# Six MLP chunks with one pair of column blocks by seven products instead of eight

## The chip, the cores and the metric

The kernel runs on one core of a Trainium2 chip. The metric is the device time of one execution in microseconds; what is given for a kernel is the median of its runs. Five engines work beside each other, each through its own instructions in order: TensorE (PE, with the loads of its stationary operand shown as PEld), VectorE (DVE), ScalarE (ACT), GpSimd (POOL) and the queue that issues the loads, SyncE (SP).

## The reference

Two layers of a decoder over 256 tokens of width 2048, float32. Layer 0 mixes tokens with a gated unit, layer 1 with windowed attention. Behind either stands an MLP, and this is what the change touches:

```
def sq_relu_mlp(x, w_up, w_down):
    return jnp.square(jax.nn.relu(x @ w_up)) @ w_down

x = layer_norm(DEEPNORM_ALPHA * x + sq_relu_mlp(x, mlp_w_up[layer], mlp_w_down[layer]), ...)
```

`w_up` is 2048 x 8192 and `w_down` 8192 x 2048. So each MLP is an up product, relu and square, and a down product, added to a multiple of `x` ahead of a layer norm.

## The kernel before

**Precision and weight tiles.** Every float32 number is split into two float32r parts, high and low, and a product is the sum of three: high x high, high x low, low x high. All weights come in tiles of 128 x 1024 numbers in the order of their use. The class `Weights` loads a tile into one of four raw places (`RAW`), ACT casts it to its high part (L95), DVE subtracts that from the raw tile for the low part (L97), and both go to a place for parts: 5 (`SLOTS`) and, from the end of the token mixer to the end of the MLP, 5 more (`EXTRA_SLOTS`). `get` splits as many tiles ahead as there are places, loads four more, and hands out the next tile; `release` gives its place back. So the splits run up to nine tiles ahead of the products, and the cast for a place waits until PE has read the tile that was there.

**The MLP.** `mlp` goes through the 8192 features in four chunks of 2048. The up product of a chunk is 8 blocks of 256 features (`col_steps`: weights stationary, activations moving; a block of both token tiles needs four weight tiles). `act` takes a block: ACT copies one half of the bank (L294), DVE adds the other (L300), one DVE instruction does relu and square (L381), and `split` writes the high part (ACT, L185) and the low part (DVE, L186) to `hT`. The down product of the chunk is four column blocks of 512 (`rows_product`: activations stationary, weights moving). Each takes 8 weight tiles, and a tile means, for each of two token tiles, two K tiles of three matmuls of 512 columns (L205 to L207), twelve in all. `residual` then adds a column block to `x` (L353). The last column block of an MLP is `last_rows`, in which the layer norm of one token tile runs beside the products of the other; the first up tiles behind a norm are `skewed` likewise.

**Order.** Program order is a hint there: apart from the loads (always in the order of the program) and the subtractions around a layer norm, the framework's scheduler places the instructions of an engine. PSUM has two double banks with the tag `mm`, for the products, and two with the tag `aux`, for transposes, the gate and the attention. Two wide buffers (`wide`, in `bc`) hold the layer norm's gains and offsets.

Of the kernel before, what the change touches and what calls it, by code (L numbers as in the profile page):

```python
# [11 lines left out]
F32 = mybir.dt.float32  # L12
# [11 lines left out]
NFC = DFF // D  # L24
# [11 lines left out]
EXTRA_SLOTS = 5  # L36
# [10 lines left out]

class Weights:
    """The weights in the order of their use: each tile [128, 1024] is loaded and split
    into two float32r parts (high + low = the float32 value) ahead of its products."""  # L50

    def __init__(self, tc, pool, tiles):
        self.tc, self.nc, self.pool, self.tiles = tc, tc.nc, pool, tiles
        self.others, self.by_pool = [], ()
        self.borrowed, self.borrowed_from = [], 0
        self.raw, self.parts, self.held = {}, {}, []
        self.n_raw = self.n_split = self.n_used = 0
        self.free = {"w": SLOTS, "extra": 0}
        self.extra, self.extra_end = None, 0
# [23 lines left out]
    def ahead(self, n_split=None):  # L83
        """Split the tiles that have a place, and load the ones after them."""
        nc = self.nc
        n_split = len(self.tiles) if n_split is None else n_split
        while self.n_split < min(n_split, len(self.tiles)):
# [4 lines left out]
            self.load(self.n_split + 1)  # L92
            raw = self.raw.pop(self.n_split)
            for s in self.pieces(self.n_split):
                nc.scalar.copy(out=hi[:, s], in_=raw[:, s])  # L95
                engine = nc.gpsimd if self.n_split in self.by_pool else nc.vector
                sub = engine.tensor_tensor(out=lo[:, s], in0=raw[:, s], in1=hi[:, s].bitcast(F32),  # L97
                                           op=ALU.subtract)
                if self.in_order:
                    self.tc.keep_in_program_order(sub)  # L100
            self.parts[self.n_split] = (hi, lo, kind)
            self.n_split += 1
    def pieces(self, n):
        """The first tile goes in halves, so that the products start early."""
        return [slice(0, TILE // 2), slice(TILE // 2, TILE)] if n == 0 else [slice(0, TILE)]

    def load(self, n):
        while self.n_raw < min(n, len(self.tiles)):
            raw = self.pool.tile([P, TILE], F32, tag="w_raw", bufs=RAW, name="w_raw")
# [7 lines left out]
    def dma(self, out, in_):  # L117
        """Loads keep the order of the program: what is used first is loaded first."""
        self.tc.keep_in_program_order(self.nc.sync.dma_start(out=out, in_=in_))

    def get(self, ahead=None):
# [3 lines left out]
        self.load(self.n_split + RAW)  # L125
# [4 lines left out]
    def release(self):  # L130
        """The oldest tile in use has been used."""
# [6 lines left out]
def trunk(ctx: ExitStack, tc: tile.TileContext, t, out):  # L138
# [8 lines left out]

    def tiles_of(name):
# [3 lines left out]
    order = []  # L152
    ends = {}
    for name in ("win_v", "win_u", "wout", "mlp0", "kv", "wq", "wo", "mlp1"):
        tiles = (mlp_order(tiles_of("up" + name[3:]), tiles_of("down" + name[3:]))
                 if name.startswith("mlp") else tiles_of(name))
        if name == "wo":
            # the last heads' rows of the first two chunks come after the other rows of both
            tiles = tiles[0:6] + tiles[8:14] + tiles[6:8] + tiles[14:]
        order += tiles  # L160
        ends[name] = len(order)
    weights = Weights(tc, wpool, order)
    weights.by_pool = range(ends["kv"] + 4, ends["wq"], POOL_EVERY)
# [20 lines left out]
    def split(dst_hi, dst_lo, src):  # L184
        nc.scalar.copy(out=dst_hi, in_=src)  # L185
        nc.vector.tensor_tensor(out=dst_lo, in0=src, in1=dst_hi.bitcast(F32), op=ALU.subtract)  # L186

# [1 line left out]
    def row_steps(stat, apart=False):  # L189
        """[tokens, 512] of both token tiles: activations stationary, weights moving.  # L190
        One step for each weight tile and token tile."""
# [6 lines left out]
        def step(i, tok, hi, lo):  # L198
            for j in range(2):
                k = 2 * i + j  # L200
                wh, wl = hi[:, j * 512:(j + 1) * 512], lo[:, j * 512:(j + 1) * 512]
                xh = stat[:, k, tok * P:(tok + 1) * P]
                xl = stat[:, k, S + tok * P:S + (tok + 1) * P]
                first, last = k == 0, k == NK - 1
# [3 lines left out]
        return ps, [partial(step, i) for i in range(NK // 2)]  # L208

    def rows_product(stat):  # L210
        ps, steps = row_steps(stat)
# [78 lines left out]
    def gather_halves(ps, bias=None):  # L290
        """The sum of the two column halves of cols_product (with a bias per feature)."""
# [514 lines left out]
```

## Time and profile before

| | before |
|---|---|
| runs, us | 2007.83, 2011.8, 2012.14 (median 2011.8) |
| profiled execution: its span, us (no other time of it is given) | 2008.3 |
| PE busy | 98% |
| DVE busy | 62% |
| ACT busy | 46% |
| mean granted TensorE clock | 0.991 |

The span runs from the first to the last instruction of the profiled execution. Matmuls are pipelined, so that PE can be busy without being at its peak: the start of one matmul against the start of the next says more than its duration. Idle time is put down to what ended it, and idle time of an engine that is not the bottleneck costs nothing.

### The profile page before, as it was taken

What the parts mean: (1) busy time and instruction counts of PE and PEld (TensorE: products, weight loads), DVE (VectorE), ACT (ScalarE), POOL (GpSimd) and SP (SyncE); (2) the same over time, 40 slices, a digit from 0 to 9 for tenths busy, and PEclk for the clock granted to TensorE, in tenths of its full rate; (3) what the DMA queues carried; (4) which work ended last, traced back from release to release, by engine and by line L of the source; (5) the groups of instructions that cost most, each with busy time, mean ns of one, the idle gap of its engine ahead of it and who ended that gap; (6) DMA issues with size and microseconds to landing.
All of it is one profiled execution on the core that took longest, in us unless ns stands there. A gap on an engine that the chain in (4) does not pass through costs nothing.

```text
span 2008.3 us, 26243 instructions
## 1 busy us (share of the span) xinstructions
PE 1963.9 (98%) x10388; PEld 1685.8 (84%) x10388; DVE 1252.5 (62%) x1345; ACT 915.5 (46%) x1138; POOL 103.1 (5%) x63
## 2 busy tenths in 40 slices
PE   9999999999999999999998889999999999999997
PEld 7888888888888888888898878888888888888886
DVE  5676686555554655564778997965555555555555
ACT  5445445434443443443456675444344344434432
POOL 0000010000000000000133310100000000000001
PEclk9999999999999999999998899999999999999999
DMA  9754846666666666655543336566676666665653
GB/s 339 259 186 151 301 143 214 189 197 224 192 192 191 187 189 194 190 184 166 179 137 107 104 106 227 175 208 190 197 228 187 194 189 189 189 194 185 189 157 104
DMA packets 105963, 377.54 MB, mean 188 GB/s; under 512 B 12272, under 2 KB 12912, under 8 KB 105840
## 3 DMA queue, kind: packets, MB, share of 16 engines
q1 hardware_dynamic: 105840, 375.86, 59.4%
q8 instruction: 81, 1.33, 0.3%
q14 instruction: 42, 0.34, 0.0%
HBM read 373.72 MB, written 2.10 MB: 187 GB/s over the span
## 4 chain that ended last, share of the span: by engine, by line
issue 82%; PE 8%; DVE 6%; ACT 2%; POOL 2%; DMA 0%; SPq 0%; POOLq 0%; ACTq 0%; DVEq 0%
PE ps_r L205 2%; PE ps_r L206 2%; PE ps_r L207 2%; DVE w_lo L97 1%; ACT p L623 1%; PE ps_c L242 1%; PE ps_c L251 1%; DVE x L332 0%; DVE swap L544 0%; POOL rstd L313 0%; DVE pT L186 0%; POOL x L328 0%; POOL x L327 0%; DVE qT L697 0%; DVE x L330 0%
## 5 line engine op out<-in xcount | busy, mean ns | idle before, releaser
L97 DVE TENSOR_TENSOR w_lo<-w_raw,w_hi 128x1024 fp32r<-128x1024 f32 (+1 forms) x655 | 803.9, 1231 | 569.7 <-ACT w_hi L95 567.7
L95 ACT CAST w_hi<-w_raw 128x1024 fp32r<-128x1024 f32 (+1 forms) x669 | 701.3, 1051 | 760.3 <-PE ps_r L207 413.4
L205 PE MATMUL ps_r<-w_hi,hT 128*128 128x512 f32 x1024 | 398.5, 389 | 0.0
L207 PE MATMUL ps_r<-w_hi,hT 128*128 128x512 f32 x1024 | 398.5, 389 | 0.0
L206 PE MATMUL ps_r<-w_lo,hT 128*128 128x512 f32 x1024 | 398.4, 389 | 0.0
L246 PE MATMUL ps_c<-yT,w_hi 128*128 128x512 f32 x960 | 337.1, 398 | 0.0
L246 PE MATMUL ps_c<-oT,w_hi 128*128 128x512 f32 x960 | 337.1, 398 | 0.0
L251 PE MATMUL ps_c<-yT,w_lo 128*128 128x256 f32 x992 | 272.5, 281 | 0.0
L251 PE MATMUL ps_c<-oT,w_lo 128*128 128x256 f32 x992 | 272.5, 281 | 0.0
L207 PEld LDWEIGHTS ps_r<-w_hi,hT 128*128 128x128 f32 x1024 | 192.2, 188 | 40.0
L206 PEld LDWEIGHTS ps_r<-w_lo,hT 128*128 128x128 f32 x1024 | 192.2, 188 | 40.0
L205 PEld LDWEIGHTS ps_r<-w_hi,hT 128*128 128x128 f32 x1024 | 192.2, 188 | 39.5
L246 PEld LDWEIGHTS ps_c<-oT,w_hi 128*128 128x128 f32 x960 | 178.7, 188 | 41.8
L246 PEld LDWEIGHTS ps_c<-yT,w_hi 128*128 128x128 f32 x960 | 178.7, 188 | 41.8
L251 PEld LDWEIGHTS ps_c<-yT,w_lo 128*128 128x128 f32 x992 | 187.4, 189 | 2.7
L251 PEld LDWEIGHTS ps_c<-oT,w_lo 128*128 128x128 f32 x992 | 187.4, 189 | 2.7
L300 DVE TENSOR_TENSOR full<-ps_c,part 128x512 f32<-128x512 f32 x73 | 50.5, 691 | 91.5 <-ACT part L294 83.7
L294 ACT COPY part<-ps_c 128x512 f32<-128x512 f32 x72 | 42.2, 587 | 131.2 <-PE ps_c L246 128.5
L242 PE MATMUL ps_c<-hT,w_hi 128*128 128x256 f32 x512 | 97.8, 294 | 0.0
L313 POOL TENSOR_TENSOR rstd<-ve,half 128x1 f32<-128x1 f32 x10 | 9.9, 987 | 1709.1 <-DVE ve L311 1709.1
L246 PE MATMUL ps_c<-xT,w_hi 128*128 128x512 f32 x256 | 90.2, 396 | 0.0
L242 PEld LDWEIGHTS ps_c<-hT,w_hi 128*128 128x128 f32 x512 | 84.4, 203 | 0.4
(141 smaller groups left out, 2026.4 us busy)
## 6 DMA issues: line engine op xcount, KB each, us to landing
w_raw<-in_up SPq DMA_DIRECT2D x256, 512.0 KB, 4.2
w_raw<-in_down SPq DMA_DIRECT2D x256, 512.0 KB, 4.1
w_raw<-in_win_u SPq DMA_DIRECT2D x32, 512.0 KB, 4.0
w_raw<-in_wout SPq DMA_DIRECT2D x32, 512.0 KB, 4.4
w_raw<-in_wq SPq DMA_DIRECT2D x32, 512.0 KB, 3.6
w_raw<-in_wo SPq DMA_DIRECT2D x32, 512.0 KB, 4.0
w_raw<-in_win_v SPq DMA_DIRECT2D x31, 512.0 KB, 6.2
b_ln_g<-in_ln_g SPq DMA_DIRECT2D x8, 512.0 KB, 5.6
```

What stands on the lines that cost most here:

```text
L95: nc.scalar.copy(out=hi[:, s], in_=raw[:, s])
L97: sub = engine.tensor_tensor(out=lo[:, s], in0=raw[:, s], in1=hi[:, s].bitcast(F32), op=ALU.subtract)
L205: nc.tensor.matmul(out=ps[tok], lhsT=xh, rhs=wh, start=first, stop=False)
L206: nc.tensor.matmul(out=ps[tok], lhsT=xh, rhs=wl, start=False, stop=False)
L207: nc.tensor.matmul(out=ps[tok], lhsT=xl, rhs=wh, start=False, stop=last)
L242: nc.tensor.matmul(out=ps[:, b, 0:S], lhsT=hi[:, w], rhs=stat[:, k, h * S:(h + 1) * S], start=first and h == 0, stop=last and h == 1)
L246: nc.tensor.matmul(out=ps[:, b, :], lhsT=hi[:, w], rhs=stat[:, k, :], start=first, stop=last)
L251: nc.tensor.matmul(out=ps[:, b, 0:S], lhsT=lo[:, w], rhs=stat[:, k, 0:S], start=False, stop=False)
L294: nc.scalar.copy(out=part, in_=ps[:, :, S:])
L300: nc.vector.tensor_tensor(out=full, in0=ps[:, :, 0:S], in1=part, op=ALU.add)
L313: nc.gpsimd.tensor_tensor(out=rstd, in0=ve, in1=half, op=ALU.pow)
L623: nc.scalar.activation(out=p[:, i, :], in_=p[:, i, :], func=AF.Exp, bias=top[:, i:i + 1], accum_out=den[:, i:i + 1])
```

## The change

`CHUNKS` cuts the 8192 features of an MLP into six chunks of 1024 and one of 2048. The last is computed as before. In the six, the columns 0 to 1023 of the down product are a product of 2 x 2 blocks: two token tiles by K tiles of even and odd number, times those K tiles by two column blocks of 512. It is done with Strassen's seven products, as Winograd arranges the sums. A `group` is four K tiles; a chunk has two. The columns 1024 to 2047 remain plain.

- `down_steps` gives the order: products 0 to 3 of both groups, then 4 to 6 of both, with a plain weight tile behind every two of them. Each product has a bank of its own of `aux`: four in the first part, three in the second.
- `add_down` says which weights make each operand. `ahead` adds raw tiles in place on DVE, one addition ahead of the subtraction, for the operand behind; four of seven operands of a group bring an addition. B11 and B12 lie in the wide buffers, B22 and B21 in the raw ring. `end` tells when a raw tile is done with.
- `act` writes four sums of the activations beside the four plain blocks (`by_pairs` gives the layout of `hT`), and relu and square are two ACT instructions. It is cut into stages, one for each following `get`.
- `evict` adds three of the products to `x` itself; four are kept in `held` (copied by ACT in the first chunk, added to by DVE in the others) and combined by `strassen_end`, one addition for each block of the last up product.
- Inside the MLP DVE and ACT keep the order of the program (`tc.manual_schedule`). `EXTRA_SLOTS` goes from 5 to 4. Loads go as far ahead as raw places are free.

The weights in memory are put in the new order on the host (`down_tiles`). Comments and docstrings are removed. The core of the diff, blank lines left out:

```diff
-EXTRA_SLOTS = 5
+CHUNKS = ((1024, 1),) * 6 + ((2048, 0),)
+EXTRA_SLOTS = 4
+STATIONARY = (0, 7, 5, 4, 6, 2, 3)
+HELD = (0, 2, 3, 4)
...
+def down_steps(groups, rounds):
+    plain = [("plain", (n, i)) for n in range(2 * rounds, 4) for i in range(2 * groups)]
+    if not rounds:
+        return plain
+    steps = []
+    for part in (range(4), range(4, 7)):
+        steps += [("strassen", (g, o)) for g in range(groups) for o in part]
+    every = -(-len(steps) // len(plain))
+    out = []
+    for i, step in enumerate(steps):
+        out.append(step)
+        if (i + 1) % every == 0 and plain:
+            out.append(plain.pop(0))
+    return out + plain
...
-            self.load(self.n_split + 1)
-            raw = self.raw.pop(self.n_split)
+            at, add, ended = self.operands[self.n_split]
+            self.load(max((at,) + (add or ())) + 1)
+            raw = self.raw[at]
             for s in self.pieces(self.n_split):
                 nc.scalar.copy(out=hi[:, s], in_=raw[:, s])
+                if add is not None:
+                    into, plus = (self.raw[n] for n in add)
+                    nc.vector.tensor_tensor(out=into, in0=into, in1=plus, op=ALU.add)
...
+            if self.homes[self.n_raw] == "w":
+                if not self.free_raw:
+                    break
+                self.free_raw -= 1
+                raw = self.pool.tile([P, TILE], F32, tag="w_raw", bufs=RAW, name="w_raw")
+            else:
+                if not self.pairs or len(self.pairs[-1][1]) == 2:
+                    if len(self.pairs) == 2:
+                        break
+                    self.pairs.append((self.wide.tile([P, 2, TILE], F32, tag="wide", name="w_wide"),
+                                       [], []))
+                pair, began, _ = self.pairs[-1]
+                raw = pair[:, len(began)]
+                began.append(self.n_raw)
...
-        self.load(self.n_split + RAW)
+        self.load(len(self.tiles))
+        for stages in self.later:
+            stages.pop(0)()
+        self.later[:] = [stages for stages in self.later if stages]
...
+    def add_down(width, rounds, down):
+        groups = width // 512
+        at = {}
+        for kind, i in down_steps(groups, rounds):
+            if kind == "plain":
+                add_tiles([down.pop(0)])
+                continue
+            g, o = i
+            for name in {0: ("B11",), 1: ("B22", "B12"), 5: ("B21",)}.get(o, ()):
+                at[g, name] = len(tiles)
+                tiles.append(down.pop(0))
+                homes.append("wide" if name in ("B11", "B12") else "w")
+            b11, b12, b22, b21 = (at.get((g, name)) for name in ("B11", "B12", "B22", "B21"))
+            operands.append([(b11, None, ()),
+                             (b22, (b11, b12), ()),
+                             (b11, (b12, b22), ()),
+                             (b12, (b11, b22), (b12, b22)),
+                             (b11, None, ()),
+                             (b21, (b11, b21), (b21,)),
+                             (b11, None, (b11,))][o])
...
+    def strassen_steps(hT, groups, n, held, first, scale):
+        own = {1: (0, 1, ALU.subtract), 5: (0, 0, ALU.add), 6: (1, 0, ALU.add)}
+        banks = {}
+        def evict(o, bank):
+            if o in own:
+                tok, c, op = own[o]
+                a = x[:, tok, (n + c) * 512:(n + c + 1) * 512]
+                nc.vector.scalar_tensor_tensor(out=a, in0=a, scalar=scale, in1=bank,
+                                               op0=ALU.mult, op1=op)
+            elif first:
+                nc.scalar.copy(out=held[:, HELD.index(o), :], in_=bank)
+            else:
+                a = held[:, HELD.index(o), :]
+                nc.vector.tensor_tensor(out=a, in0=bank, in1=a, op=ALU.add)
+            if o == 6 and scale != 1.0:
+                a = x[:, 1, (n + 1) * 512:(n + 2) * 512]
+                nc.scalar.mul(out=a, in_=a, mul=scale)
+        def step(g, o):
+            if o not in banks:
+                two = psum.tile([P, 2, 512], F32, tag="aux", name="ps_s")
+                banks[o], banks[o + 1] = two[:, 0, :], two[:, 1, :]
+            hi, lo = weights.get()
+            for j in range(2):
+                k = 2 * g + j
+                wh, wl = hi[:, j * 512:(j + 1) * 512], lo[:, j * 512:(j + 1) * 512]
+                xh, xl = (hT[:, k, part, STATIONARY[o], :] for part in range(2))
+                start, stop = k == 0, k == 2 * groups - 1
+                nc.tensor.matmul(out=banks[o], lhsT=xh, rhs=wh, start=start, stop=False)
+                nc.tensor.matmul(out=banks[o], lhsT=xh, rhs=wl, start=False, stop=False)
+                nc.tensor.matmul(out=banks[o], lhsT=xl, rhs=wh, start=False, stop=stop)
+            weights.release()
+            if g == groups - 1:
+                evict(o, banks[o])
+        return step
...
+    def strassen_end(n, held):
+        m1, m5, m7, m6 = (held[:, i, :] for i in range(4))
+        (x11, x12), (x21, x22) = ([x[:, tok, (n + c) * 512:(n + c + 1) * 512] for c in range(2)]
+                                  for tok in range(NT))
+        for out, a, b, op in ((m6, m6, m1, ALU.subtract), (x11, x11, m1, ALU.add),
+                              (x21, x21, m6, ALU.subtract), (x21, x21, m7, ALU.add),
+                              (m5, m6, m5, ALU.subtract), (x12, x12, m5, ALU.add),
+                              (x22, x22, m5, ALU.add), (x22, x22, m7, ALU.subtract)):
+            yield partial(nc.vector.tensor_tensor, out=out, in0=a, in1=b, op=op)
...
+        for fc, (width, rounds) in enumerate(CHUNKS):
+            last = fc == len(CHUNKS) - 1
             def act(c, ps):
-                full = gather_halves(ps)
-                nc.vector.scalar_tensor_tensor(out=full, in0=full, scalar=0.0, in1=full,
-                                               op0=ALU.max, op1=ALU.mult)
-                split(hT[:, 2 * c:2 * c + 2, 0:S], hT[:, 2 * c:2 * c + 2, S:], full)
+                part = work.tile([P, 2, S], F32, tag="part", name="part")
+                nc.scalar.copy(out=part, in_=ps[:, :, S:])
+                full = work.tile([P, 2, S], F32, tag="full", name="full")
+                def gather():
+                    nc.vector.tensor_tensor(out=full, in0=ps[:, :, 0:S], in1=part, op=ALU.add)
+                    if not rounds:
+                        nc.vector.scalar_tensor_tensor(out=full, in0=full, scalar=0.0, in1=full,
+                                                       op0=ALU.max, op1=ALU.mult)
+                if not rounds:
+                    hi, lo = (hT[:, 2 * c:2 * c + 2, i * S:(i + 1) * S] for i in range(2))
+                    weights.later.append([gather, partial(high, hi, full), partial(low, lo, full, hi)])
+                    return
+                a = full.rearrange("p b (t q) -> p (b t) q", t=NT)
+                his, los = ([hT[:, c, i, h:h + 4] for h in (0, 4)] for i in range(2))
+                sums = []
+                def square():
+                    nc.scalar.activation(out=full, in_=full, func=AF.Relu)
+                    nc.scalar.activation(out=full, in_=full, func=AF.Square)
+                def add():
+                    b = work.tile([P, 4, P], F32, tag="part", name="sums")
+                    nc.vector.tensor_tensor(out=b[:, 0:2], in0=a[:, 0:4:3],
+                                            in1=a[:, 1:2].to_broadcast([P, 2, P]), op=ALU.subtract)
+                    nc.vector.tensor_tensor(out=b[:, 2], in0=a[:, 0], in1=b[:, 1], op=ALU.add)
+                    nc.vector.tensor_tensor(out=b[:, 3], in0=b[:, 2], in1=a[:, 2], op=ALU.subtract)
+                    high(his[0], a)
+                    sums.append(b)
+                def both():
+                    high(his[1], sums[0])
+                    low(los[0], a, his[0])
+                    low(los[1], sums[0], his[1])
+                weights.later.append([gather, square, add, both])
...
+            with tc.manual_schedule(engines={mybir.EngineType.DVE, mybir.EngineType.Activation}):
+                if fc == 0:
+                    for c in range(c0):
+                        act(c, heads[c][0])
+                for c in range(c0, width // 256):
+                    act(c, cols_product(xT))
+                    if ends:
+                        ends.pop(0)()
...
+                strassen, rows = None, {}
+                if rounds:
+                    first = held is None
+                    if first:
+                        held = extra.tile([P, 4, 512], F32, name="held")
+                    strassen = strassen_steps(hT, width // 512, 0, held, first, scale)
+                for kind, i in down_steps(width // 512, rounds):
+                    if kind == "strassen":
+                        strassen(*i)
+                        continue
+                    n, i = i
+                    if n == 3 and last:
+                        break
+                    if n not in rows:
+                        rows[n] = row_steps(stat, nk=width // P)
+                    hi, lo = weights.get()
+                    for tok in range(NT):
+                        rows[n][1][i](tok, hi, lo)
+                    weights.release()
+                    if i == width // 256 - 1:
+                        residual(x, rows[n][0], n, stats if last else None, scale)
+                if rounds and not any(r for _, r in CHUNKS[fc + 1:]):
+                    ends += strassen_end(0, held)
```

## Rows read from the trace of the kernel before

**Rows 1.** The core view: span in us, mean granted TensorE clock.

```profile
core 0: 2008.3 us, clock 0.991
```

**Rows 2.** The page's first part: busy us, share of the span, instructions.

```profile
PE 1963.9 (98%) x10388; PEld 1685.8 (84%) x10388; DVE 1252.5 (62%) x1345; ACT 915.5 (46%) x1138; POOL 103.1 (5%) x63
```

**Rows 3.** Windows of two products: us; busy PE, PEld, DVE, ACT, POOL; clock, DMA share, GB/s.

```profile
462.64:553.04 90.40, 90.40 (x514) 78.45 (x512) 53.44 (x55) 41.12 (x46) 0.00 (x0) 1.00 0.67 210
553.04:640.10 87.06, 87.06 (x385) 72.07 (x384) 44.68 (x41) 34.85 (x34) 0.00 (x0) 1.00 0.65 193
```

**Rows 4.** The timeline of PE in a down product: start, duration, instruction.

```profile
629.22 0.39 PE L205 MATMUL ps_r<-w_hi,hT 128*128 128x512 f32 x1
...
631.94 0.39 PE L205 MATMUL ps_r<-w_hi,hT 128*128 128x512 f32 x1
```

**Rows 5.** The waits of the span: who waited for whom, us, times, longest.

```profile
DVE w_lo L97 <- ACT w_hi L95: 567.7, 398, 5.1
ACT w_hi L95 <- PE ps_r L207: 413.4, 237, 15.3
ACT w_hi L95 <- PE ps_c L246: 241.9, 139, 1.8
...
ACT w_hi L95 <- DMA w_raw<-in_up: 10.4, 12, 1.4
...
PE ps_p L639 <- POOL p L629: 7.7, 4, 3.1
...
ACT w_hi L95 <- DMA w_raw<-in_down: 6.0, 7, 2.0
```

**Rows 6.** Groups by line and shape: busy us, mean ns; idle before.

```profile
L97 DVE TENSOR_TENSOR w_lo<-w_raw,w_hi 128x1024 fp32r<-128x1024 f32 x653 | 802.6, 1233 | 567.5 <-ACT w_hi L95 565.6
L95 ACT CAST w_hi<-w_raw 128x1024 fp32r<-128x1024 f32 x667 | 700.1, 1052 | 758.3 <-PE ps_r L207 413.4 <-PE ps_c L246 241.9 <-DMA w_raw<-in_win_v 25.6
...
L353 DVE SCALAR_TENSOR_TENSOR x<-x,ps_r 128x512 f32<-128x512 f32 x80 | 51.9, 683 | 40.0 <-PE ps_r L207 40.0
...
L300 DVE TENSOR_TENSOR full<-ps_c,part 128x512 f32<-128x512 f32 x73 | 50.5, 691 | 91.5 <-ACT part L294 83.7 <-ACT part L297 7.8
...
L186 DVE TENSOR_TENSOR hT<-full,hT 128x512 fp32r<-128x512 f32 x64 | 43.8, 685 | 1.4 <-ACT hT L185 1.4
L294 ACT COPY part<-ps_c 128x512 f32<-128x512 f32 x72 | 42.2, 587 | 131.2 <-PE ps_c L246 128.5 <-PE ps_c L238 2.6
L185 ACT CAST hT<-full 128x512 fp32r<-128x512 f32 x64 | 39.8, 622 | 32.2 <-DVE full L381 32.2
...
L610 DVE TENSOR_TENSOR p<-sc,mask 128x1024 f32<-128x1024 f32 x12 | 14.7, 1223 | 7.0 <-PE sc L605 6.7
...
L662 DVE TENSOR_TENSOR o<-ps_o,part_o 64x256 f32<-64x256 f32 x16 | 6.7, 416 | 2.8 <-ACT part_o L661 2.6
...
L499 DVE TENSOR_TENSOR y<-sg,uT 128x512 f32<-128x512 f32 x8 | 5.4, 684 | 0.0
```

**Rows 7.** The timeline of DVE behind a norm: four subtractions.

```profile
295.96 4.62 DVE L97 TENSOR_TENSOR w_lo<-w_raw,w_hi 128x1024 fp32r<-128x1024 f32 x4
```

**Rows 8.** The timeline of PE and DVE where an up product ends.

```profile
552.81 0.39 PE L246 MATMUL ps_c<-yT,w_hi 128*128 128x512 f32 x1
...
553.04 0.39 PE L205 MATMUL ps_r<-w_hi,hT 128*128 128x512 f32 x1
...
556.38 0.69 DVE L186 TENSOR_TENSOR hT<-full,hT 128x512 fp32r<-128x512 f32 x1
```

**Rows 9.** The page's DMA issues: count, KB, median us to landing.

```profile
w_raw<-in_down SPq DMA_DIRECT2D x256, 512.0 KB, 4.1
```

**Rows 10.** Groups of DVE's instructions in the up product.

```profile
L97 DVE TENSOR_TENSOR w_lo<-w_raw,w_hi 128x1024 fp32r<-128x1024 f32 x32 | 39.2, 1224 | 27.3 <-ACT w_hi L95 27.2
```

**Rows 11.** The timeline of DVE in the first up product, behind the norm.

```profile
314.82 1.23 DVE L97 TENSOR_TENSOR w_lo<-w_raw,w_hi 128x1024 fp32r<-128x1024 f32 x1 [0.46 <-ACT w_hi L95]
317.66 1.23 DVE L97 TENSOR_TENSOR w_lo<-w_raw,w_hi 128x1024 fp32r<-128x1024 f32 x1 [1.61 <-ACT w_hi L95]
```

More of the change, by code (lines that the diff above doesn't have):

```diff
@@ L85, in ahead @@
         nc = self.nc
-        n_split = len(self.tiles) if n_split is None else n_split
-        while self.n_split < min(n_split, len(self.tiles)):
+        n_split = len(self.operands) if n_split is None else n_split
+        while self.n_split < min(n_split, len(self.operands)):
             place = self._place(self.n_split)
@@ L100, in ahead, with end @@
                     self.tc.keep_in_program_order(sub)
+            for n in ended:
+                self.end(n)
             self.parts[self.n_split] = (hi, lo, kind)
             self.n_split += 1
+    def end(self, n):
+        self.raw.pop(n)
+        if self.homes[n] == "w":
+            self.free_raw += 1
+            return
+        for pair in self.pairs:
+            if n in pair[1]:
+                pair[2].append(n)
+        self.pairs = [pair for pair in self.pairs if len(pair[2]) < 2]
     def pieces(self, n):
@@ L146, in trunk, with add_tiles @@
     psum = ctx.enter_context(tc.tile_pool(name="psum", bufs=2, space=bass.MemoryType.PSUM))
+    tiles, homes, operands = [], [], []
+    ends = {}
+    def add_tiles(new):
+        for w in new:
+            tiles.append(w)
+            homes.append("w")
+            operands.append((len(tiles) - 1, None, (len(tiles) - 1,)))
+    def add_down(width, rounds, down):
[18 more added lines that the diff above has]
+                             (b11, None, (b11,))][o])
     def tiles_of(name):
@@ L150, in tiles_of @@
         return [w[i] for i in range(w.shape[0])]
-    order = []
-    ends = {}
     for name in ("win_v", "win_u", "wout", "mlp0", "kv", "wq", "wo", "mlp1"):
[L155 to L162, printed above, removed]
+        if name.startswith("mlp"):
+            up, down = tiles_of("up" + name[3:]), tiles_of("down" + name[3:])
+            for width, rounds in CHUNKS:
+                n_up = width * D // (P * TILE)
+                add_tiles(up[:n_up])
+                del up[:n_up]
+                add_down(width, rounds, down)
+        else:
+            some = tiles_of(name)
+            if name == "wo":
+                some = some[0:6] + some[8:14] + some[6:8] + some[14:]
+            add_tiles(some)
+        ends[name] = len(operands)
+    weights = Weights(tc, wpool, bc, tiles, homes, operands)
     weights.by_pool = range(ends["kv"] + 4, ends["wq"], POOL_EVERY)
@@ L370, in borrow @@
     def borrow(tag, first):
-        if first < len(order):
+        if first < len(operands):
             weights.borrow(big.tile([P, 4, 2, TILE], F32R, tag=tag, name="lent"), first)
-    def mlp(x, xT, norm, loads, tags, end):
+    def strassen_steps(hT, groups, n, held, first, scale):
[9 more added lines that the diff above has]
+                nc.scalar.copy(out=held[:, HELD.index(o), :], in_=bank)
+            else:
+                a = held[:, HELD.index(o), :]
[20 more added lines that the diff above has]
+        return step
@@ L385, in mlp @@
             c0 = 0
[L386 removed]
+            if last:
                 loads()
@@ L391, in mlp @@
                 skewed([f for _, steps in heads for f in steps], HEAD_LEAD, turn_at=HEAD_TURNS)
-            hT = big.tile([P, NK, 2 * S], F32R, tag=h_tag, name="hT")
-            if fc == 0:
-                for c in range(c0):
-                    act(c, heads[c][0])
-            for c in range(c0, NK // 2):
-                act(c, cols_product(xT))
-                if c == 2:
-                    weights.in_order = False
-            if fc == NFC - 1:
-                borrow(x_tag, end)
-            for n in range(4):
-                st = stats if fc == NFC - 1 else None
-                scale = ALPHA if fc == 0 else 1.0
-                if n == 3 and fc == NFC - 1:
-                    last_rows(x, hT, st, scale, partial(norm, stats, hT), end < len(order))
-                else:
-                    residual(x, rows_product(hT), n, st, scale)
+            shape = [P, width // 256, 2, 8, P] if rounds else [P, NK, 2 * S]
@@ L411, in trunk @@
+            if last:
+                last_rows(x, hT, stats, scale, partial(norm, stats, hT), end < len(operands))
     cos = const.tile([P, S], F32, name="cos")
```

84 lines of the change are left out of this document (54 added, 30 removed).

## Prediction

> **What bounds the kernel now.** I read the core view first, for the span: 2008.3 us, clock 0.991 [rows 1]. Timed runs gave 2007.83, 2011.8 and 2012.14, so this span lies 0.5 us above the fastest and 3.5 us below the median; the sum below is made on the span, and the 3.5 us are carried over. The page's first part has PE busy for 98% of it, VectorE (DVE) for 62%, ScalarE (ACT) for 46% [rows 2]. A busy PE need not be a full one, so I went to the stretches: in the MLP one up product of 2048 features takes 90.40 us and the down product behind it 87.06 us, PE busy in all of it, clock 1.00 [rows 3]. Inside a down product the matmuls of 512 columns start every 0.227 us, twelve to a weight tile (629.22 to 631.94) [rows 4], and 384 of them at that pace make 87.1 us, the whole stretch. So there is no hole there, and one matmul less is worth 0.2267 us (87.06/384) for as long as the others keep their pace. An up product has 512 matmuls in 90.40 us, 0.1766 each. The waits say the same from the other side: ACT's casts wait 413.4 and 241.9 us for PE to free a weight place, DVE waits 567.7 us for ACT, and PE's longest wait for anybody totals 7.7 us, in the attention [rows 5]. The order is PE, then ACT, then DVE: PE is the bound, and DVE has room.
>
> **What the change takes from PE.** Before, 1024 rows of a down product cost 16 weight tiles of 12 matmuls, 192. After, columns 0 to 1023 of such a chunk go as 7 products for 2 groups, 14 operands of 6 matmuls, 84 instead of 96; columns 1024 to 2047 remain 8 plain tiles, 96. That is 180 against 192. There are 6 such chunks in each of 2 MLPs: 12 x 12 = 144 matmuls fewer, 144 x 0.2267 = 32.6 us. Up products keep count and shape. Each matmul has its own weight load before and after, and both operand kinds run the same (high, high, low) triple, so I keep 0.2267 us for a Strassen matmul: 1.36 us an operand, 2.72 us a plain tile. A chunk is then 45.2 us of up (256 x 0.1766) and 40.8 us of down (180 x 0.2267), 86.0 us, against 88.7 before.
>
> **What it adds on DVE and ACT.** Per chunk, by rows of the same shape [rows 6]: the subtraction for the low part, 38 operands (16 up, 8 plain, 14 Strassen) where there were 32 tiles, 38 x 1.233 = 46.9 us; 8 additions of weight tiles, new. For these the trace has no row with both inputs of 1024 in SBUF; bounds are 1.22 us (the same size with one input in PSUM) and twice the 512-column add in SBUF, 1.37 us. I take 1.22, since size sets the rows here: 9.8 us. Sums of activations, three small additions in each of 4 blocks: one of 256 columns at 0.42 us and two of 128 at no more than that, so between 0.4 and 1.3 us a block; I take 1.0: 4 us. Low parts, two a block instead of one, 8 x 0.685 = 5.5; gathers 4 x 0.691 = 2.8; seven evictions of a bank at 0.69 = 4.8; residual 4 x 0.684 = 2.7. Sum 76.5 us of DVE in 86.0 us of PE, where it was 49 in 88.7 (half of both stretches) [rows 3]. ACT: 38 casts of 1.05 us, and a copy, a relu, a square and two casts per block at 0.59 to 0.62, some 52 us. Relu and square on ACT replace one DVE instruction of 0.69 us. Both engines fit on the average, DVE closely.
>
> An average isn't enough, because the work is uneven: in the down part an operand lasts only 1.36 us on PE and needs 1.23 us, or 2.45 with an addition, on DVE. What bridges this is the lead: 9 places, one in use, so at operand n the splits are for n + 8. DVE then does in the up part 16 splits and 4 additions besides 3 blocks, about 34 us in 45.2; in the down part 22 splits (14 left of this chunk, 8 of the next up part), 4 additions, one block, 7 evictions and 4 residuals, 42.5 us against 40.8. By start-to-start times it is less: four subtractions in a row took 4.62 us, 1.155 each [rows 7], 6% under their mean duration, so about 40 us. DVE falls a few us behind and recovers in the next up part; a lead of 8 operands is 14 us of PE. Weights are not late.
>
> Three things could be. **The last pair of the up product**: before, the down product began 0.2 us after the last up matmul, while the last block's low part came 4 us later [rows 8], and was wanted only at tile 8, 19 us on. Now group 1 wants it at the seventh operand, 10.9 us after the start, and its matmuls on that pair only 0.7 us later still. I add up DVE's queue from there in the order of the code, at start-to-start times (1.15 for 1024 columns, 0.62 for 512): the up part leaves it 1.3 us late, as its last operand asks for an addition, a subtraction and two low parts; the next cast is done at 1.75. Subtraction and gather 1.85, twice addition and subtraction 4.55, sums 1.0, subtraction 1.1, two low parts 1.25: the end is at 11.5. The first matmul that reads the low part of the plain activations (written 0.6 us before the end, at 10.9) is at 12.0; the one that reads the low part of the sums at 13.4. Margins 1.1 and 1.9 us. **The banks**: part two of the products wants banks 0 and 1 at operand 13, 21.8 us; their evictions end near 18.4. Banks 2 and 3 are wanted at 27.2 and free near 24.2. **The loads**: bytes do not change, a tile lands in 4.1 us [rows 9] and 4 places remain, of which B22 holds one for four operands more. Its place is next asked for by a plain tile which is split 12 us later; only the first up tiles of the next chunk come close, and they are used 8 operands on. DMA was busy at 0.65 [rows 3].
>
> Edits that cost nothing, with their cover: additions of the held products at the end, 8 x 0.69 us, one to a block of the last up product, where DVE idles 27.2 of 90 us for ACT's casts alone [rows 10]. The additional ends of chunks: PE passes from one product to the next in 0.23 us. Program order on DVE and ACT: each waits for PE in the order in which PE comes anyway; what queues behind an eviction is the split for 8 operands on. If the cover fails, this is the second case below. One place for parts less (9 for 10): the head after the norm gets its lead back by about 317 us, where DVE waits for ACT again in the steady rhythm [rows 11], and the first down part would begin near 330 us; I put 0 to 3 us for each of two heads and tails, and take 1 in all, as PE there stands for the norm and not for weights. Sum: -32.6 + 1 = -31.6, span 1976.7, median about 1980.
>
> **Rivals.** (1) DVE's queue comes late by its own rule. For it: margins of 1.1 to 3.4 us on sums of a dozen instructions. If each instruction occupies the queue for its full duration, not the start-to-start time, the low part of the pair ends at about 12.5 instead of 11.5; with one hand-over more of ACT (0.6) or one step of 2.45 in between, PE waits 0.5 to 2.2 us in each of 12 chunks, 6 to 26 us. Against it: [rows 7]. I put 15 us: 1995. The Trainium skill (VectorE: DVE Perf Modes, The DRAIN you can't avoid) says that a VectorE instruction doesn't start until the pipe of the one before is empty, which would put the spacing at the duration; the trace disagrees, 1.155 against 1.233 us.
>
> (2) The lead isn't there when a down part begins, because a place in the raw ring, a load or a wait on ACT holds the splits, and DVE must do the chunk's own operands in its own down part: 22 x 1.233 + 8 x 1.22 + 3 for a block + 7.5 for the evictions = 47.4 us, which then sets it, against 43.5 us of PE before. Plus 3.9 a chunk, 12 times: +47, 2059. It decides once the lead is under two or three operands (each carries 1.2 to 2.4 us). For it: DVE goes from 49 to 76 us per chunk, in one order, with chains add - cast - subtract over two engines. Against it: 11 us of free DVE in each up part, and no wait for a load of up or down weights above 2.0 us [rows 5].
>
> (3) Half of that: the lead holds at first and wears off, and waits eat the 32 us: within 4 us of before.
>
> (4) The removed matmuls are not worth their spacing, for instance if operands of six let PE run dry at each hand-over. The rows show none at hand-overs every 2.72 us [rows 4]; no chance of its own, it is in (1).
>
> **How the numbers follow.** Forecast 0.66, with 1973 to 1987; (1) 0.20, from 1987 to 2007; (3) 0.05; (2) 0.09. A measurement here tells about 0.2%, 4 us, from no change. Faster 0.86, same 0.05, slower 0.09. Range: 1973 (all 32.6 us, from a run 6 us lower than the median's sum would give) to 2000, which takes in some two thirds of (1): 0.66 + 0.13 = 0.79.
>
> **What would show it.** Right: 40.8 us from the first to the last matmul of a Strassen down part, spacing 0.227 throughout; no wait of PE for hT or for a bank; DVE above 80% in the MLP, its idle time before subtractions down from 567.7 us to under 250, and behind PE only in down parts. Rival (1): a gap of PE at the seventh operand of each down part, ended by a low part of hT, or at the thirteenth by an eviction. Rival (2): PE waits for w_lo, with DVE without a hole. Wrong altogether: spacing above 0.23 us inside operands, or a lower granted clock.

## The result and the profile after

The changed kernel takes 1985.58 us (median of four runs, 1984.76 to 1986.99); before, measured beside it, 2011.67. The ratio is 0.9875 with a 95% interval of [0.9861, 0.9889]: 26.1 us less, where 31.6 were forecast; the forecast time was about 1980, and 1985.58 lies inside the range. The profiled execution has a span of 1983.0 us, 25.3 less than [rows 1], and a time of 1984.76, so 1.8 us lie around the span.

The page's first part, which answers to [rows 2]:

```profile
span 1983.0 us, 26631 instructions
PE 1936.6 (98%) x10244; PEld 1656.8 (84%) x10244; DVE 1524.4 (77%) x1749; ACT 1064.8 (54%) x1364; POOL 102.5 (5%) x63
```

144 matmuls are gone and PE is as busy as before. One up part and one down part of a Strassen chunk, in the windows view with the columns of [rows 3]:

```profile
372.80:418.00 45.20, 45.20 (x258) 39.22 (x256) 32.98 (x40) 24.97 (x31) 0.00 (x0) 1.00 0.64 207
418.00:459.36 41.36, 41.36 (x181) 33.56 (x180) 37.80 (x42) 24.30 (x27) 0.00 (x0) 1.00 0.53 171
```

The up part is what 256 matmuls should take. The down part has its 180 matmuls and is 0.54 us longer than the 40.82 they should take; over the twelve chunks of the trace the excess is 0.35 to 0.69 us, 5.3 in all. PE's busy time doesn't show it, as PE is busy for all 41.36 us. The weight loads (PEld) do, as theirs are the waits: the waits view of PEld in the down parts and up parts of the first MLP, 331 to 896 us, where the kernel before has none:

```profile
PEld ps_s L525 <- DVE held L510: 3.7, 13, 0.4
PEld ps_s L525 <- ACT held L507: 0.7, 2, 0.3
PEld ps_s L527 <- DVE hT L294: 0.4, 1, 0.4
```

Products wait for evictions (the first two lines), and once for a low part of hT. The timeline at one of them, 16 us into the down part (start, duration, engine, instruction, in brackets the idle time and what ended it):

```profile
434.16 0.68 DVE L510 TENSOR_TENSOR held<-ps_s,held 128x512 f32<-128x512 f32 x1
...
434.34 0.39 PE L324 MATMUL ps_r<-w_hi,hT 128*128 128x512 f32 x1
...
434.57 0.39 PE L325 MATMUL ps_r<-w_lo,hT 128*128 128x512 f32 x1
...
434.90 0.19 PEld L525 LDWEIGHTS ps_s<-w_hi,hT 128*128 128x128 f32 x1 [0.37 <-DVE held L510]
434.90 0.50 PE L525 MATMUL ps_s<-w_hi,hT 128*128 128x512 f32 x1
...
435.24 0.40 PE L526 MATMUL ps_s<-w_lo,hT 128*128 128x512 f32 x1
...
436.61 0.69 DVE L504 SCALAR_TENSOR_TENSOR x<-x,ps_s 128x512 f32<-128x512 f32 x1 [0.63 <-PE ps_s L527]
```

DVE evicts product 0 (held) until 434.84, and only then PE begins product 1 of group 1, the one that goes to `x` at 436.61. These two lie in one double tile of PSUM, in different banks. Two things are to be seen. PE's order isn't two products and a plain tile here: two matmuls of a plain tile stand before the product, and ten behind it. Only DVE and ACT keep the program's order; that of PE is the framework's scheduler's. What remains is a hole of 0.1 us, and it costs twice that: the starts at 434.57, 434.90 and 435.24 are 0.33 and 0.34 us apart instead of 0.227.

The new instructions, by line and shape (busy us, mean ns, idle before):

```profile
L133 DVE TENSOR_TENSOR w_wide<-w_wide,w_raw 128x1024 f32<-128x1024 f32 x72 | 87.8, 1219 | 0.8
...
L294 DVE TENSOR_TENSOR hT<-sums,hT 128x512 fp32r<-128x512 f32 x48 | 32.8, 683 | 0.0
L576 ACT ACTIVATE full<-full 128x512 f32<-128x512 f32 x48 | 30.4, 633 | 1.5
...
L510 DVE TENSOR_TENSOR held<-ps_s,held 128x512 f32<-128x512 f32 x40 | 27.3, 682 | 0.0
...
L580 DVE TENSOR_TENSOR sums<-full 128x256 f32<-128x256 f32 x48 | 20.1, 418 | 0.0
...
L583 DVE TENSOR_TENSOR sums<-sums,full 128x128 f32<-128x128 f32 x48 | 14.0, 292 | 1.6
```

The addition of weight tiles takes 1.219 us (1.22 was put), the three small sums 1.0 us a block (1.0).

### The profile page after: what moved, and what is told of

The parts are those of the page before. It is cut to its first block, busy times and chain, and to the rows that moved or that the text cites. A ratio compares the mean times of both kernels' runs of the same rounds, so it can differ in the third digit from the quotient of the medians.

```text
span 1983.0 us, 26631 instructions
## 1 busy us (share of the span) xinstructions
PE 1936.6 (98%) x10244; PEld 1656.8 (84%) x10244; DVE 1524.4 (77%) x1749; ACT 1064.8 (54%) x1364; POOL 102.5 (5%) x63
## 4 chain that ended last, share of the span: by engine, by line
issue 82%; PE 9%; DVE 6%; ACT 2%; POOL 1%; DMA 0%; SPq 0%; POOLq 0%; ACTq 0%; DVEq 0%
PE ps_r L326 2%; PE ps_r L324 2%; PE ps_r L325 2%; PE ps_c L361 1%; DVE w_lo L135 1%; PE ps_c L370 1%; ACT p L856 1%; DVE x L451 0%; POOL rstd L432 0%; DVE pT L294 0%; POOL x L447 0%; DVE qT L930 0%; POOL x L446 0%; DVE x L449 0%; DVE top L847 0%
## 5 line engine op out<-in xcount | busy, mean ns | idle before, releaser
L135 DVE TENSOR_TENSOR w_lo<-w_raw,w_hi 128x1024 fp32r<-128x1024 f32 (+1 forms) x607 | 739.7, 1230 | 340.0 <-ACT w_hi L130 337.5
L130 ACT CAST w_hi<-w_raw 128x1024 fp32r<-128x1024 f32 (+1 forms) x621 | 645.6, 1049 | 513.2 <-PE ps_c L365 167.9
L324 PE MATMUL ps_r<-w_hi,hT 128*128 128x512 f32 x640 | 249.2, 389 | 0.0
L326 PE MATMUL ps_r<-w_hi,hT 128*128 128x512 f32 x640 | 249.1, 389 | 0.0
L325 PE MATMUL ps_r<-w_lo,hT 128*128 128x512 f32 x640 | 249.0, 389 | 0.0
L135 DVE TENSOR_TENSOR w_lo<-w_wide,w_hi 128x1024 fp32r<-128x1024 f32 x120 | 146.3, 1219 | 30.5 <-ACT w_hi L130 30.4
L130 ACT CAST w_hi<-w_wide 128x1024 fp32r<-128x1024 f32 x120 | 125.9, 1051 | 75.5 <-DVE w_wide L133 39.9
L325 PEld LDWEIGHTS ps_r<-w_lo,hT 128*128 128x128 f32 x640 | 120.1, 188 | 25.1
L326 PEld LDWEIGHTS ps_r<-w_hi,hT 128*128 128x128 f32 x640 | 120.1, 188 | 25.0
L324 PEld LDWEIGHTS ps_r<-w_hi,hT 128*128 128x128 f32 x640 | 120.2, 188 | 24.8
L525 PE MATMUL ps_s<-w_hi,hT 128*128 128x512 f32 x336 | 131.8, 397 | 0.0
L527 PE MATMUL ps_s<-w_hi,hT 128*128 128x512 f32 x336 | 131.3, 391 | 0.0
L526 PE MATMUL ps_s<-w_lo,hT 128*128 128x512 f32 x336 | 131.2, 391 | 0.0
```

The costliest lines, as they stand in the source:

```text
L324: nc.tensor.matmul(out=ps[tok], lhsT=xh, rhs=wh, start=first, stop=False)
L325: nc.tensor.matmul(out=ps[tok], lhsT=xh, rhs=wl, start=False, stop=False)
L326: nc.tensor.matmul(out=ps[tok], lhsT=xl, rhs=wh, start=False, stop=last)
L525: nc.tensor.matmul(out=banks[o], lhsT=xh, rhs=wh, start=start, stop=False)
L526: nc.tensor.matmul(out=banks[o], lhsT=xh, rhs=wl, start=False, stop=False)
L527: nc.tensor.matmul(out=banks[o], lhsT=xl, rhs=wh, start=False, stop=stop)
```

## The experiments

Each kernel is the changed one with one edit, except where it says otherwise. "Down part" means the 180 matmuls of a Strassen chunk, 40.82 us at [rows 4]'s pace, 41.36 in the chunk above. The interval behind a ratio is the 95% one, against the kernel before.

**Own PSUM tiles.** Four tiles of one bank in place of two of two:

```diff
-                two = psum.tile([P, 2, 512], F32, tag="aux", name="ps_s")
-                banks[o], banks[o + 1] = two[:, 0, :], two[:, 1, :]
+                banks[o] = aux.tile([P, 512], F32, tag="one", name="ps_s")
```

(`aux` is a pool that holds four single banks between the two ends of an MLP and two double ones elsewhere.)

> Each of the seven products gets a PSUM tile of one bank for itself, four such tiles, where before two products shared a tile of two banks; banks, order and work are else the same. Theory A (the 0.4 us lost in each Strassen down part come from a product of group 1 that waits until the eviction of the other product in its double tile is done, although that lies in the other bank): PE's waits on the evictions, 3.7 + 0.7 us in the first MLP and 3.0 + 0.5 in the second, go; the steps come back to two products and a plain tile, and a chunk takes 86.0 us instead of 86.4, the span 1983 - 5 = 1978. Rival B (DVE is late at that point whatever is shared): the wait goes to the next thing that DVE owes, a low part of hT or the bank for part two; chunk at 86.3 to 86.6, span 1982 to 1984.

Measured: 1980.87 us, ratio 0.9849 [0.9836, 0.9863], span 1978.8. The chunk that follows the first of an MLP, with the columns of [rows 3]:

```profile
373.16:418.36 45.20, 45.20 (x257) 39.23 (x256) 33.67 (x41) 25.80 (x32) 0.00 (x0) 1.00 0.63 211
418.36:459.18 40.82, 40.82 (x181) 33.78 (x180) 37.96 (x42) 24.40 (x27) 0.00 (x0) 1.00 0.55 176
```

All ten down parts behind the first of each MLP are 40.82 us, those two 41.06 and 41.12. No wait for an eviction is left in PEld's waits; of hT there are two of 0.4 us, in the first chunks. In the chunk shown PE's order is two products and a plain tile again. Theory A holds: it was the shared tile, not the bank and not DVE's lateness as such. The down parts show it better than the span: they are 4.8 us shorter in all. The first up parts are 0.9 and 1.3 us longer than in the changed kernel (51.07 and 51.83 us against 50.13 and 50.48; more on them at the last runs), and stages that are the same in both kernels are some 1.7 us shorter, so it is in part luck that the span fell by 4.2 where 5 were expected. The Trainium skill (PSUM — Partial Sum Buffer, PSUM bank collisions raise a hardware error) asks for a guard by bank and 32 partitions; the double tile was guarded more coarsely than that, and with a guard by bank the evictions run beside products in other banks at no cost here.

**The chunks without Strassen.**

```diff
-CHUNKS = ((1024, 1),) * 6 + ((2048, 0),)
+CHUNKS = ((1024, 0),) * 6 + ((2048, 0),)
```

> The same six chunks of 1024 features, program order, stages and places, but all four column blocks of the down product plain: 16 tiles of 12 matmuls. Theory A (the gain is the 144 matmuls at 0.2267 us, and nothing else): 32.6 us less the 5.4 of holes above the changed kernel, chunk of 45.2 + 43.5 = 88.7 us, span 1983 + 27 = 2010, so within 3 us of before, the rest being the head's and the attention's 2 us. Rival B (chunks, stages or program order pay or cost something by themselves): 2000 or under, or 2018 and over.

Measured: 2015.78 us, ratio 1.0023 [1.0014, 1.0032], span 2013.2, 4.9 above before, and so between the two theories' ranges. One chunk:

```profile
376.00:421.20 45.20, 45.20 (x257) 39.22 (x256) 26.21 (x27) 20.13 (x22) 0.00 (x0) 1.00 0.60 187
421.20:464.94 43.74, 43.74 (x194) 35.97 (x193) 25.00 (x25) 17.97 (x18) 0.00 (x0) 1.00 0.61 192
```

The 192 matmuls take 43.74 us and not 43.53: the last pair of the up product is wanted at the fourth tile and is late (PEld waits 0.3 us for hT in each of six chunks). That is 0.2 a chunk; the first four blocks behind the two norms are 4 us longer in all (51.07 and 51.76 us against 49.04 and 49.70 before; see the last runs). So small chunks cost a little. The kernel with own tiles has the same at these places within 0.1 us, and its span is 34.4 us shorter than this one's. That is what the seven products pay: 12 x (43.74 - 40.82) = 35.

**The additions twice**, in the changed kernel and in the one with own tiles:

```diff
+                    nc.vector.tensor_tensor(out=lo, in0=into, in1=plus, op=ALU.add)
                     nc.vector.tensor_tensor(out=into, in0=into, in1=plus, op=ALU.add)
```

> Every addition of two weight tiles on DVE is preceded by a second one of the same size that writes to the place of the low part, where the subtraction overwrites it: 8 more DVE instructions of 1.22 us in a chunk, 9.2 us by start-to-start times, on top of some 71 in 86. Theory A (DVE has room on the average, and what it owes in the down part early is near its limit): the low parts of the last pair come 2.3 us later, 13.8 where 12.0 to 13.4 is asked, evictions 4 us later; PE waits 1 to 3 us in each chunk, span 1995 to 2020. Rival B (DVE is far from the path, the lead takes all of it): within 3 us of 1983. Rival C (DVE is the bound already): 12 x 9.2, span near 2090.

> A PSUM tile of one bank for each product, and each addition of two weight tiles done twice, as in the run that doubled them (which took 4.9 us a chunk: PE waited up to 3.6 us for the low part of a plain tile). Theory A (that loss came from the shared double tiles: products of group 1 wait for an eviction, PE's order has plain tiles ahead of them, and these use up the lead): with own tiles PE keeps the order of two and one, DVE at some 80 us of 86 is still covered, waits are under 1 us a chunk, for the last pair; span 1980 to 1992. Theory B (DVE itself can't carry 9 us more in this order): 4 to 5 us a chunk as before, span 2030 to 2040.

Measured: 2044.34 us, ratio 1.017 [1.0156, 1.0184], for the changed kernel; 2002.61, ratio 0.9956 [0.9942, 0.997], with own tiles. Three down parts of the former (the first without its last product, which PE did behind the first up matmul):

```profile
422.34:468.35 46.01, 42.88 (x176) 34.66 (x175) 40.98 (x45) 21.57 (x25) 0.00 (x0) 0.93 0.38 126
514.68:561.74 47.06, 43.94 (x181) 35.55 (x180) 42.23 (x46) 22.70 (x26) 0.00 (x0) 0.93 0.40 133
606.94:651.60 44.66, 41.53 (x181) 33.51 (x180) 40.96 (x45) 21.59 (x25) 0.00 (x0) 1.00 0.42 135
```

and where the time goes in the first, in the timeline:

```profile
441.56 0.39 PE L325 MATMUL ps_r<-w_hi,hT 128*128 128x512 f32 x1
442.67 2.35 DVE L136 TENSOR_TENSOR w_lo<-w_raw,w_hi 128x1024 fp32r<-128x1024 f32 x2
...
444.94 0.68 DVE L511 TENSOR_TENSOR held<-ps_s,held 128x512 f32<-128x512 f32 x1
...
445.08 0.80 PE L326 MATMUL ps_r<-w_lo,hT 128*128 128x512 f32 x1 [3.13 <-DVE w_lo L136]
...
445.67 0.63 PE L327 MATMUL ps_r<-w_hi,hT 128*128 128x512 f32 x1
```

PE had gone ahead into a plain tile while a product waited for its eviction, and the plain tile's low part stood in DVE's queue ahead of that eviction: 3.1 us without a matmul. The loss is 4.9 us a chunk, above theory A's 1 to 3 and below the 9 that DVE as the bound (C) would cost. With own tiles a down part is 42.2 to 44.1 us; PEld's waits in the first MLP:

```profile
PEld ps_s L547 <- ACT hT L314: 10.6, 12, 1.6
PEld ps_r L348 <- DVE w_lo L136: 4.7, 5, 0.9
```

Here neither theory hit the size: A said under 1 us a chunk, B 4 to 5; it is 2.1 on the mean of twelve. Both parts are real. The shared tiles make up more than half of the loss in the changed kernel (58.8 us there, 21.7 with own tiles), and with 9 us more on DVE the last pair is late twice a chunk by 0.9 us, the step that the prediction put near its limit; it is the high part (a cast of ACT, behind DVE's sums) that comes last. DVE is busy for 70.78 of 86.56 us in a chunk of the changed kernel, so there seems to be room; yet 13% more work for it costs 21.7 us with own tiles (1980.87 to 2002.61), over two thirds of that kernel's gain of 30.3.

**Plain tiles last.**

```diff
-        if (i + 1) % every == 0 and plain:
-            out.append(plain.pop(0))
```

> In each of the six chunks the eight plain tiles stand behind all fourteen Strassen operands instead of one behind every two. Work, counts and places are the same. Theory A (the plain tiles give DVE the time that the operands of 1.36 us don't): the last pair of the up product is wanted at 5.4 us instead of 10.9 and DVE has it at 10.5 by the same sum, and part two wants its banks at once; PE waits 5 to 8 us in each chunk, span 2040 to 2080, slower than before. Rival B (the lead of eight operands covers it in any order): span under 1990.

Measured: 2085.86 us, ratio 1.037 [1.0354, 1.0385]: slower than before by 75 us, a little more than A's range. One down part, with the columns of [rows 3], and PE's waits in it:

```profile
426.73:475.44 48.71, 44.44 (x181) 34.50 (x180) 38.02 (x42) 25.32 (x27) 0.00 (x0) 0.93 0.60 192
```

```profile
PE ps_s L523 <- DVE held L508: 2.3, 1, 2.3
PE ps_s L523 <- ACT hT L289: 1.2, 1, 1.2
PE ps_s L523 <- DVE x L502: 0.4, 1, 0.4
PE ps_s L525 <- DVE hT L292: 0.4, 1, 0.4
```

These are the two debts named, the pair and the banks. The products still share double tiles here, so the waits for banks may hold some of that kind. The four waits make 4.3 of the 7.9 us above 40.82; the granted clock is 0.93 there, and what it takes of the rest was not separated. Without the plain tile behind every two products the change doesn't pay.

**A shorter lead.** In the six chunks splits run three operands ahead:

```diff
+        ahead = self.lead if ahead is None else ahead
         self.ahead(None if ahead is None else n + 1 + ahead)
...
+            weights.lead = 3 if rounds else None
```

> The changed kernel, but in the six chunks splits run at most three operands ahead of the products instead of eight. Theory A (the lead carries DVE over the down part): DVE must then do 22 splits, 7 or 8 additions, a block and the evictions in the 40.8 us of the down part, 44.7 us by start-to-start times, with 5 us of cover; PE waits for low parts of weights, 1 to 5 us a chunk, span 1995 to 2040. Rival B (the order alone suffices, three are enough): within 4 us of 1983.

Measured: 2013.12 us, ratio 1.0011 [1.0001, 1.002]. A down part, and PE's waits for weights in the first MLP:

```profile
419.80:463.47 43.67, 42.00 (x182) 33.63 (x180) 42.24 (x46) 25.24 (x27) 0.00 (x0) 1.00 0.51 159
```

```profile
PE ps_r L327 <- DVE w_lo L136: 5.9, 10, 0.6
PE ps_s L527 <- ACT w_hi L131: 2.7, 11, 0.3
```

With a lead of three the gain is gone, whatever PE saves, which is theory A: the down part takes what half a down product took before (43.5 us). Rival (2) put the point at which this decides at two or three operands.

**No program order.** The `with tc.manual_schedule(...)` becomes `if True`.

> The changed kernel without the program order on DVE and ACT in the MLP: the framework's scheduler places their instructions, as it did before the change. Theory A (program order keeps splits, stages and evictions in the order in which PE asks for them; DVE has some 15 us of room a chunk, but an eviction or a low part that is placed behind several splits costs PE its lateness): 1 to 4 us a chunk more, span 1995 to 2030. Rival B (order doesn't matter as long as DVE has room): within 4 us of 1983.

Measured: 1983.89 us, ratio 0.9865 [0.985, 0.9879], span 1983.0 as with program order. Down parts are 40.96 to 41.15 us instead of 41.17 to 41.51, 1.9 less in all, and the first up parts 2.3 us longer in all (51.07 and 51.80). Rival B holds: program order on DVE and ACT gains nothing here.

**Before, with four additional places**, and **own tiles with five**, the held products in one of them:

```diff
-EXTRA_SLOTS = 5
+EXTRA_SLOTS = 4
```

```diff
-EXTRA_SLOTS = 4
+EXTRA_SLOTS = 5
...
+        if kind == "extra" and self.keep:
+            self.keep = False
+            self.kept = [self.extra.tile([P, TILE], F32, tag=f"w_{part}", bufs=EXTRA_SLOTS,
+                                         name="held") for part in ("hi", "lo")]
```

> The kernel before the change with 4 instead of 5 additional places for parts, nothing else. Theory A (the first up part, 1.1 and 0.8 us longer in the changed kernel, pays for the place that went to the held products): first up parts of 95.0 to 96.5 us where they take 94.2 and 94.9, span 2009.5 to 2012. Rival B (the head pays for program order or for its stages): up parts unchanged within 0.3 us, span within 0.5 of 2008.3.

> Own PSUM tiles of one bank, as in the first run, and five additional places for parts again: the four held products lie in the high and low part of one of these places, which is taken when it is next released behind the norm and given back after the last combination. So the norm's head has ten places, the chunks nine. Theory A (the head's 2.0 and 2.1 us in the run of own tiles, and in the kernel before with four places, are the fifth place's): first up parts of 49.0 and 49.7 us instead of 51.1 and 51.8, down parts unchanged at 40.8, span 1978.8 - 4 = 1975. Rival B (the stages of the first blocks, which run with two blocks at once behind the norm, cost the head): head within 0.5 us of the run of own tiles, span 1978 to 1980.

Measured: before with four places 2012.91 us, ratio 1.0008 [0.9999, 1.0018], span 2011.0; own tiles with five 1974.94 us, ratio 0.9818 [0.9805, 0.9832], span 1973.7. The first four blocks of the first MLP, behind the norm, in the windows of before, of before with four places, of the changed kernel and of own tiles with five:

```profile
281.34:330.38 49.04, 47.65 (x340) 44.41 (x338) 38.00 (x44) 21.63 (x27) 4.16 (x3) 1.00 0.57 183
```

```profile
280.14:331.21 51.07, 48.99 (x339) 45.94 (x338) 38.15 (x44) 22.31 (x28) 4.16 (x3) 0.97 0.57 175
```

```profile
281.16:331.29 50.13, 47.67 (x339) 44.43 (x338) 41.15 (x53) 26.47 (x36) 4.16 (x3) 1.00 0.51 179
```

```profile
280.88:329.93 49.05, 47.67 (x340) 44.43 (x339) 41.27 (x53) 25.77 (x35) 4.16 (x3) 1.00 0.48 172
```

It goes with the fifth place and not with the stages (theory A in both runs; with four places the whole first up parts of before are 96.27 and 96.96 us, the second a little above the range given). The loss has two levels, about 1 us at clock 1.00 and 2 us at 0.97; why the clock falls in some of these kernels and not in others was not tried. The last kernel is the best of all. Its span is 34.6 us below [rows 1]: the forecast's 32.6 us, and 2.0 more. The latter isn't shown to be the change's: nearly all of it lies between the start of the last down product of the first MLP and the first matmul of the attention's output product, a stretch with the same products in both kernels (258.8 us against 260.6).

## Why the prediction was right, and where its size was off

- **What leaves PE.** Right to the digit once nothing else stands in the way: 180 matmuls in 40.82 us against 40.8, 0.2267 each, up parts 45.20 against 45.2. Rival (4), that they aren't worth their spacing, is out.
- **The load on DVE and ACT.** DVE is busy for 70.8 us in a chunk and ACT for 49.3; the sums by durations gave 76.5 and 52. DVE is busy for 82% of the chunk (above 80% was forecast). Reading DVE by start-to-start times was right, though the prediction's 1.155 us is a little too long, as four subtractions in a row show here as well:

```profile
445.77 4.62 DVE L135 TENSOR_TENSOR w_lo<-w_raw,w_hi 128x1024 fp32r<-128x1024 f32 x4
```

The 4.62 us run from the first one's start to the last one's end, so that with durations of 1.22 the starts are 1.13 apart. The Trainium skill (VectorE: DVE Perf Modes, The DRAIN you can't avoid) says that the next instruction awaits the pipe's end, and in the same paragraph that one which is not held starts earlier. The prediction left the second half out; the first half alone is not what this trace shows. For the addition of weight tiles the prediction missed a row: the subtraction in [rows 6] has both inputs of 1024 columns in SBUF too, at 1.233 us (measured for the addition: 1.219). The forecast that DVE's wait before subtractions falls under 250 us was wrong:

```profile
DVE w_lo L135 <- ACT w_hi L130: 367.9, 308, 8.1
ACT w_hi L130 <- DMA w_raw<-in_up: 107.5, 109, 3.2
```

The second line is something that the prediction took lightly: ACT's casts wait 107.5 us for loads of up weights, where it was 10.4 [rows 5]. PE doesn't wait for weights in the MLP, so the lead covers it; whether it is what keeps DVE's wait so long was not tried.

- **The banks, priced at nothing: the term that was mis-sized.** I took a product to be ready when its own bank was evicted, and so looked at operand 13 only, with 3.4 us of margin. DVE came about when I said (the evictions of banks 0 and 1 end 16.8 and 19.3 us after the start; 18.4 was put); but products waited for the other half of their double tile, two or three times a chunk: products 1 and 3 of group 1, and one of part two. Of the 5.3 us of holes in twelve chunks, 4.8 go with own tiles; the other 0.5 is the last pair's. It is a wait for DVE, as in rival (1), but at another place, by another cause, and for a third of its price. Whether PE's reordered sequence kept it so small was not tried.
- **The last pair.** In time, as computed (the end of its low parts was put at 11.5 us and is at 11.6 in the chunk above), except in the first chunk of each MLP, where PE's weight load waits 0.4 us. The margin of 1 to 2 us was real: without two more plain tiles ahead (plain tiles last), or with 2.3 us more before it (additions twice), it is late.
- **The lead.** Right, and the point where it decides too: three operands give 2013.12, no gain. Two were not tried.
- **The heads.** Put at 1 us, they cost 1.1 and 0.8 for the fifth place. With the holes that is 7.2 of the 7.3 us between 32.6 and the 25.3 measured on the span. That it comes out so closely is luck: the stages that the change doesn't touch differ by up to 2 us from kernel to kernel and nearly cancel here.

## What to carry to other kernels

A change that takes matmuls from a saturated PE pays by their spacing, if the engine that prepares operands is counted by stretch and not by its average: what decides here is the lead and what stands between short operands. Give each accumulation that is evicted by itself a PSUM tile of its own; in this kernel a double tile made two banks wait as one. When something is paid for with a buffer place, look at the stage where places are scarce, not where the new thing runs.

## What the runs showed of the hardware

A wait of PE can cost more than its length. In the run with doubled additions a 3.1 us wait was followed by matmuls 0.43 us apart (445.67 to 446.10, 446.53) where they had been 0.23. The granted clock before and behind the wait, with the columns of [rows 3]:

```profile
439.00:441.90 2.90, 2.90 (x13) 2.06 (x11) 2.87 (x4) 1.39 (x2) 0.00 (x0) 1.00 0.59 181
445.00:449.00 4.00, 3.92 (x9) 3.14 (x10) 1.76 (x3) 0.00 (x0) 0.00 (x0) 0.50 0.74 253
```

That is the upper of the two clocks (2.4 GHz) before it and the lower (1.2 GHz) behind it. Of the three down parts shown of that run, the second and the third have the same 180 matmuls; PE is idle for 3.1 us in either (the first column less the second), but the second takes 47.1 us at a mean granted clock of 0.93, the third 44.7 at 1.00. So the same idle time lowered the clock in one of them and not in the other. And at clock 1.00, in the changed kernel, a hole of 0.1 us in PE's stream cost 0.2, as the matmul behind the hole (434.90) is 0.34 us from the next instead of 0.227.
